# First modulation of a hybrid block: all four quarters as two TensorE rows

## The chip, the cores and the metric

The kernel runs on one core of a Trainium2 chip. The metric is the device time of one execution in microseconds (us); a lower time is better. The engines named below are PE (TensorE), DVE (VectorE), ACT (ScalarE), POOL (GpSimd) and SP (SyncE, whose queue issues the DMAs here).

## What is computed

The block works on 2048 latent tokens and 256 context tokens of width 1024. Before anything else each token is normalised and modulated; the shift and the scale are rows of 1024 numbers made from a conditioning vector, one vector `c` for the latents and one, `c_ctx`, for the context:

```python
ml = jnp.split((jax.nn.silu(c) @ p["mod_w"] + p["mod_b"])[:, None, :], 6, axis=-1)
mc = jnp.split(jax.nn.silu(c_ctx) @ p["mod_w"] + p["mod_b"], 6, axis=-1)
zl = modulate(rms_norm(xl, p["norm1_g"]), ml[0], ml[1]) @ p["w_in"]
zc = modulate(rms_norm(xc, p["norm1_g"]), mc[0], mc[1]) @ p["w_in"]
# modulate(h, shift, scale) = h * (1 + scale) + shift
```

`zl` and `zc` feed three groups of mixers (gated linear attention, a delta-rule recurrence, retention). Their outputs go through one output projection, a second normalisation and a squared-ReLU MLP. All inputs are float32.

## The kernel before

**First modulation (`modulation1`).** It needs the first 2048 columns of `mod_w`, a 1024 by 2048 matrix, in four quarters of 512 columns. Eight DMAs of 1 MB each bring them into the tiles `mw`, two for each quarter. `cs` holds SiLU of both conditioning vectors, two columns for each of the eight slices of 128 rows. Quarters 0 and 1 are the shift, quarters 2 and 3 the scale.

For quarters 0 and 1 PE multiplies the eight slices by the two columns at once (L199), which gives a tile `pm` of two rows (latents and context; one buffer); DVE adds the bias (L201, tile `mrow`), and a product with a selector `msel` (L202) spreads one of the rows over all 128 partitions (tile `pb`), from where ACT copies it to `b1r` (L203). For quarters 2 and 3 the latents go another way: DVE multiplies each of the eight slices of `mw` by its column of `cs` and adds them up in `macc` (L208, L210), and PE sums `macc` over the partitions with a matrix of ones (L211), on top of a bias product (L205). For the context, PE multiplies the same slices by a column repeated 128 times (L214). In all cases DVE then makes `m1r = (1 + scale) * g` (L219) and takes the largest absolute value of each half row (L220, tile `mx`).

From these maxima `h_factors` (L245 to L247) makes `h_s`, a number by which each normalised token is multiplied before it is split into two float16 parts.

**Token tiles (`h_stats`, `h_block`).** There are 18 tiles `x` of 128 tokens in five blocks, taken in the order block 1 (4 tiles, latents), block 0 (2 tiles, context), blocks 2, 3 and 4 (4 tiles each). At most 12 `x` are in memory. For each tile: a DMA brings `x` (L305), ACT takes the sum of squares (L307), DVE makes the reciprocal roots of a block in 13 small steps (L310, then L140 to L146), POOL (for two tiles of the first block DVE) multiplies by `m1r` (L324), DVE multiplies by the root and adds `b1r` (L325), ACT makes the float16 part `hi` with `h_s` (L328), DVE the rest `lo` (L329), and two transposing DMAs put both into the tensors `hT_hi` and `hT_lo` (L330, L331).

**Input projection (`ip_block`).** For each of three column groups L, G and k0 and each block, PE sums 24 products into `pz` (L425), of which there are two buffers, and ACT copies `pz` to `zs` (L428), which SP stores. The weights are split in the same way (`ip_weights`, L356 to L363).

**After that** come features, a long scan (roughly 600 to 2050 us), whose PE instructions are recorded by one helper line (L1068) and into which matrix products of the rest of the input projection (`pz<-rwh,rh`, `pz<-rwl,rh`) are laid as filling, then the output projection and the MLP.

**What sets the order.** Each engine executes its instructions in program order. That order isn't the order of the source: the tile framework places the instructions of all engines by a timeline that it works out at build time (L2278), so a change at the start of the program can move instructions anywhere behind it. `issue_after` adds a wait on another instruction.

Of the kernel before, what the change touches and what calls it, by code (L numbers as in the profile page):

```python
# [11 lines left out]
F32 = mybir.dt.float32  # L12
# [5 lines left out]
ALU = mybir.AluOpType  # L18
# [4 lines left out]
P = 128  # L23
D = 1024
KD = D // P
# [124 lines left out]
def modulation1(k, xp, pp, then):  # L150

    nc, tc, I = k.nc, k.tc, k.I
    cp = k.cpool
    k.cs = cs = cp.tile([P, KD, 2], F32, name="cs")
    k.h_inv = cp.tile([P, 2], F32, name="h_inv")
    k.hs = cp.tile([P, 2], F32, name="h_s")
    k.b1r = [xp.tile([P, D], F32, name=f"b1r{s}", bufs=1) for s in range(2)]
    k.m1r = [xp.tile([P, D], F32, name=f"m1r{s}", bufs=1) for s in range(2)]
    with tc.tile_pool(name="mo1", bufs=1, side="right") as m1, tc.tile_pool(name="mo2", bufs=1, side="right") as mp:
        mw = I["mod_w"].rearrange("o (k p) n -> p (o k) n", p=P)  # L160
        k.ident = cp.tile([P, P], F32, name="ident")
        make_identity(nc, k.ident)
        cr = m1.tile([16, P], F32, name="crows")
        nc.sync.dma_start(cr[0:8], I["c"].rearrange("o (r p) -> (o r) p", p=P))
        nc.sync.dma_start(cr[8:16], I["c_ctx"].rearrange("(r p) -> r p", p=P))
        mb = mp.tile([2, 2 * D], F32, name="mbrow")
        nc.sync.dma_start(mb, I["mod_b"][:, 0 : 2 * D].to_broadcast([2, 2 * D]))
        ws = []
        for q in range(4):
            for kk in range(0, KD, 4):  # L170
                w = (m1 if q < 2 else mp).tile([P, 4, 512], F32, tag="mw", name="mw", bufs=4)
                nc.sync.dma_start(w, mw[:, kk : kk + 4, 512 * q : 512 * q + 512])
                ws += [w[:, i] for i in range(4)]
        g = xp.tile([P, D], F32, name="mrowg", bufs=1)
        nc.sync.dma_start(g, I["norm1_g"].to_broadcast([P, D]))
        ones = k.ones = cp.tile([P, P], F32, name="ones")
        nc.gpsimd.memset(ones, 1.0)
        sel = m1.tile([2, 2, P], F32, name="msel")
        nc.gpsimd.tensor_copy(sel, k.ident[0:2, 0:2].unsqueeze(2).to_broadcast([2, 2, P]))
        pc = pp.tile([P, 2, KD], F32, tag="pc", name="pc", bufs=1)  # L180
        nc.tensor.transpose(pc.rearrange("p i r -> p (i r)"), cr, k.ident[0:16, 0:16])
        th = m1.tile([P, 2, KD], F32, name="sil")
        nc.scalar.activation(th, pc, AF.Tanh, scale=0.5)
        nc.vector.tensor_scalar(th, th, 0.5, 0.5, ALU.mult, ALU.add)
        nc.vector.tensor_tensor(cs.rearrange("p r i -> p i r"), th, pc, ALU.mult)
        mx = xp.tile([P, 2, 4], F32, name="mx", bufs=1)
        mm = xp.tile([P, 2, 2], F32, name="mxx", bufs=1)
        rows = {}

        def rows_of(s):  # L190
            todo = []
            for q in range(4):
                hf, mq = slice(512 * (q % 2), 512 * (q % 2) + 512), mb[:, 512 * q : 512 * q + 512]
                pb = pp.tile([P, 512], F32, tag="pb", name="pb")
                if q < 2:
                    if s == 0:
                        pm = pp.tile([2, 512], F32, tag="pm", name="pm", bufs=1)
                        for kk in range(KD):
                            nc.tensor.matmul(pm, cs[:, kk, :], ws[KD * q + kk], start=(kk == 0), stop=(kk == KD - 1))  # L199
                        rows[q] = m1.tile([2, 512], F32, tag="row", name="mrow", bufs=2)  # L200
                        nc.vector.tensor_tensor(rows[q], pm, mq, ALU.add)  # L201
                    nc.tensor.matmul(pb, sel[:, s], rows[q], start=True, stop=True)  # L202
                    nc.scalar.copy(k.b1r[s][:, hf], pb)  # L203
                else:
                    nc.tensor.matmul(pb, ones[0:1], mq[0:1], start=True, stop=False)  # L205
                    if s == 0:
                        acc = mp.tile([P, 512], F32, tag="macc", name="macc", bufs=2)
                        nc.vector.tensor_scalar(acc, ws[KD * q], cs[:, 0, 0:1], None, ALU.mult)  # L208
                        for kk in range(1, KD):
                            nc.vector.scalar_tensor_tensor(acc, ws[KD * q + kk], cs[:, kk, 0:1], acc, ALU.mult, ALU.add)  # L210
                        k.m_last = nc.tensor.matmul(pb, ones, acc, start=False, stop=True).ins  # L211
                    else:
                        for kk in range(KD):
                            nc.tensor.matmul(pb, cs[:, kk, 1:2].to_broadcast([P, P]), ws[KD * q + kk], start=False, stop=(kk == KD - 1))  # L214

                def rest(q=q, hf=hf, pb=pb):
                    r = (k.b1r if q < 2 else k.m1r)[s][:, hf]
                    if q >= 2:
                        nc.vector.scalar_tensor_tensor(r, pb, 1.0, g[:, hf], ALU.add, ALU.mult)  # L219
                    nc.vector.tensor_reduce(mx[:, s, q : q + 1], r, axis=AX.X, op=ALU.max, apply_absolute_value=True)  # L220

                if s == 0:
                    rest()
                else:
                    todo.append(rest)

            def factors():
                for f in todo:
                    f()
                nc.vector.tensor_reduce(mm[:, s], mx[:, s].rearrange("p (a b) -> p a b", a=2), axis=AX.X, op=ALU.max)  # L230
                h_factors(nc, mm[:, s, 1:2], mm[:, s, 0:1], k.h_inv[:, s : s + 1], k.hs[:, s : s + 1])

            return factors

        rows_of(0)()
        then()
        first = h_stats(k, TOK_ORDER[0], xp)
        with tc.issue_after(k.m_last):
            rest = rows_of(1)
    return first, rest  # L240


def h_factors(nc, m, b, h_inv, hs):

    nc.vector.tensor_scalar(h_inv, m, 32.0, b, ALU.mult, ALU.add)  # L245
    nc.vector.tensor_scalar(h_inv, h_inv, 1e-30, 2.0 ** -14, ALU.max, ALU.mult)
    nc.vector.reciprocal(hs, h_inv)  # L247
# [2034 lines left out]
```

## Time and profile before

| | us |
|---|---|
| three runs | 3601.03, 3632.33, 3631.42 |
| median | 3631.42 |
| profiled execution, time | 3641.55 |
| profiled execution, span from first to last instruction | 3639.4 |
| PE busy | 3362.6 (92%) |
| DVE busy | 2388.7 (66%) |
| ACT busy | 1427.0 (39%) |
| POOL busy | 685.8 (19%) |
| mean granted PE clock | 0.913 |

Busy times say how long an engine had an instruction in work. The granted clock is the share of full speed that PE was allowed in a stretch: 1.00 is 2.4 GHz, 0.50 is 1.2 GHz. In the rows further down, a timeline row gives the start, the time in us, the engine, the line, the operation with its output and inputs, how many instructions were merged (x4), and in brackets how long the engine had been idle and what released it. An instruction that had to wait for something inside its engine shows that wait as part of its time.

### The profile page before, as it was taken

The numbers are of one execution on the slowest core, as the hardware profiler recorded it, in microseconds if no ns is written. First come the engines' busy times: TensorE is split into PE (matmuls) and PEld (weight loads), VectorE is DVE, ScalarE is ACT, GpSimd is POOL, SyncE is SP. The second block draws the span as 40 slices with busy tenths as digits, with TensorE's granted clock in tenths as the row PEclk, the third lists the DMA queues.
The fourth block names the chain that finished last, engine by engine and source line by source line (L and its number), as shares of the span: only waits on it lengthen the run. The fifth ranks groups of instructions, "written<-read, shape, count | busy, mean of one in ns | idle before, by whom it ended". The sixth has DMA issues, their size and how long they took to land. (4 is left out here: it accounts for less than half of the span.)

```text
span 3639.4 us, 62904 instructions
## 1 busy us (share of the span) xinstructions
PE 3362.6 (92%) x23600; PEld 2257.2 (62%) x23600; DVE 2388.7 (66%) x5128; ACT 1427.0 (39%) x3161; POOL 685.8 (19%) x863
## 2 busy tenths in 40 slices
PE   6798999998998999999999689799999999999997
PEld 2444445666675667777676577556666666666665
DVE  7458784767865667666656378777777764454446
ACT  3355553444434464443434234444433441122113
POOL 3224442324522223323222100000000010000001
PEclk7898999999987988778998599899999999999998
DMA  7988877536645245242523168744433473232232
GB/s 229 201 242 247 251 213 209 162 99 194 167 140 135 78 126 147 68 110 92 151 77 102 57 195 229 241 176 142 172 141 136 155 228 116 90 118 93 90 102 89
DMA packets 534345, 547.09 MB, mean 150 GB/s; under 512 B 276603, under 2 KB 407494, under 8 KB 533262
## 3 DMA queue, kind: packets, MB, share of 16 engines
q1 hardware_dynamic: 534032, 542.99, 50.1%
q8 instruction: 188, 3.08, 0.3%
q14 instruction: 125, 1.02, 0.1%
HBM read 331.18 MB, written 187.55 MB: 143 GB/s over the span
## 5 line engine op out<-in xcount | busy, mean ns | idle before, releaser
L1938 PE MATMUL pu<-H,wo 128*128 128x512 f16 x2688 | 608.7, 380 | 1.2 <-DVE s L1946 1.2
L2125 DVE TENSOR_TENSOR acc<-acc,pz 128x512 f32<-128x512 f32 x512 | 348.6, 686 | 348.3 <-PE pz L2123 346.5
L1938 PEld LDWEIGHTS <-wo 128*128 128x128 f16 x2688 | 252.0, 98 | 320.4 <-issue 41.1
L2123 PE MATMUL pz<-w2h,uh 128*128 128x512 f32 x1024 | 425.2, 419 | 11.7 <-ACT uh L1965 10.5
L2123 PE MATMUL pz<-w2l,uh 128*128 128x512 f32 x1024 | 403.4, 394 | 0.0
L2123 PE MATMUL pz<-w2h,ul 128*128 128x512 f32 x1024 | 397.3, 391 | 0.4 <-DVE ul L1967 0.4
L1068 PE MATMUL pz<-rwh,rh 128*128 128x384 f16 (+1 forms) x1376 | 294.5, 345 | 12.6 <-DMA rh<-hd 6.2
L1068 PEld LDWEIGHTS <-rh 128*128 128x128 f16 x2064 | 200.9, 106 | 137.8 <-issue 37.0
L2139 POOL TENSOR_TENSOR acc<-acc,fg 128x1024 f32<-128x1024 f32 x10 | 23.6, 2377 | 1373.9 <-ACT acc L2138 1373.9
L2123 PEld LDWEIGHTS pz<-w2h,uh 128*128 128x128 f32 x1024 | 194.0, 189 | 65.6 <-ACT uh L1965 11.5
L2123 PEld LDWEIGHTS pz<-w2h,ul 128*128 128x128 f32 x1024 | 192.9, 188 | 42.8 <-DVE ul L1967 1.1
L2123 PEld LDWEIGHTS pz<-w2l,uh 128*128 128x128 f32 x1024 | 194.2, 190 | 40.1
L425 PEld LDWEIGHTS <-wh 128*128 128x128 f16 (+2 forms) x1072 | 111.5, 108 | 148.5 <-issue 40.8
L1962 ACT ACTIVATE u<-u 128x512 f32<-128x512 f32 x64 | 36.8, 623 | 402.9 <-DVE s L1956 402.9
L425 PE MATMUL pz<-hT_hi,wh 128*128 128x512 f16 (+5 forms) x536 | 125.1, 374 | 41.4 <-ACT zs L428 23.5
L1068 PE MATMUL pz<-rwl,rh 128*128 128x384 f16 (+1 forms) x688 | 146.1, 343 | 0.0
L1068 PE MATMUL pg<-Z,BK 64*128 64x128 f32 (+1 forms) x864 | 131.3, 329 | 3.8 <-issue 1.1
L1950 ACT ACTIVATE s<-pu,iv 128x512 f32<-128x512 f32 x96 | 65.2, 684 | 166.3 <-PE pu L1938 163.9
L2043 PE MATMUL pz<-woh,yh 128*128 128x512 f32 x256 | 100.9, 409 | 30.7 <-DMA x<-in_w_out_dram 22.0
L425 PE MATMUL pz<-hT_hi,wl 128*128 128x512 f16 (+5 forms) x536 | 123.4, 368 | 0.0
L425 PE MATMUL pz<-hT_lo,wh 128*128 128x512 f16 (+5 forms) x536 | 121.4, 365 | 0.0
L1068 PEld LDWEIGHTS pg<-Z,BK 64*128 64x128 f32 x864 | 111.4, 226 | 15.0 <-issue 6.9
(522 smaller groups left out, 6920.4 us busy)
## 6 DMA issues: line engine op xcount, KB each, us to landing
rh<-hd SPq DMA_DIRECT2D x86, 512.0 KB
st<-in_mlp_w_dram SPq DMA_DIRECT2D x64, 512.0 KB
w1d<-wo SPq DMA_DIRECT2D x112, 256.0 KB
wo<-w1d SPq DMA_DIRECT2D x112, 256.0 KB
x<-in_x_dram SPq DMA_DIRECT2D x32, 512.0 KB
mw<-in_mod_w_dram SPq DMA_DIRECT2D x32, 512.0 KB
w2d<-w2h SPq DMA_DIRECT2D x32, 512.0 KB
w2d<-w2l SPq DMA_DIRECT2D x32, 512.0 KB
```

Of the source, the lines that this page charges most:

```text
L425: nc.tensor.matmul(pz[:M, o : o + step], a[:, kk, 0:M], b[:, kk, t0 + o : t0 + o + step], start=(i == 0), stop=(i == 23))
L1068: return op(out, lhs, rhs, **kw)
L1938: nc.tensor.matmul(bank, W[o][:, a, kk], H[o][:, 4 * b + kk], start=(i == 0), stop=(i == 11))
L1950: nc.scalar.activation(s, product(o), AF.Copy, scale=iv)
L1962: nc.scalar.activation(r, r, AF.Relu)
L2043: nc.tensor.matmul(pz, a[:, kk], w[:, kk, 512 * hf : 512 * hf + 512], start=(kk + i == 0), stop=(kk == KD - 1 and i == 2))
L2123: nc.tensor.matmul(pz, U[q][tb][u][:, ts], W2[q][w][:, cs], start=(i == 0), stop=(i == 5))
L2125: nc.vector.tensor_add(a[:, cs], a[:, cs], pz)
L2139: nc.gpsimd.tensor_mul(a, a, fg)
```

## The change

All four quarters now take the way of quarters 0 and 1: PE makes two rows, DVE adds the bias, and PE spreads the row over the partitions, for latents and for context. The accumulation on DVE (L208, L210), the sum by ones (L211), the bias products (L205) and the context products (L214) are gone. `mrow` has four buffers in place of two; `pm` still has one. `k.m_last`, the instruction behind which the rows of the context are issued, is now the spreading product of quarter 3.

```diff
                 hf, mq = slice(512 * (q % 2), 512 * (q % 2) + 512), mb[:, 512 * q : 512 * q + 512]
+                if s == 0:
+                    pm = pp.tile([2, 512], F32, tag="pm", name="pm", bufs=1)
+                    for kk in range(KD):
+                        nc.tensor.matmul(pm, cs[:, kk, :], ws[KD * q + kk], start=(kk == 0), stop=(kk == KD - 1))
+                    rows[q] = m1.tile([2, 512], F32, tag="row", name="mrow", bufs=4)
+                    nc.vector.tensor_tensor(rows[q], pm, mq, ALU.add)
                 pb = pp.tile([P, 512], F32, tag="pb", name="pb")
+                k.m_last = nc.tensor.matmul(pb, sel[:, s], rows[q], start=True, stop=True).ins
                 if q < 2:
-                    if s == 0:
-                        pm = pp.tile([2, 512], F32, tag="pm", name="pm", bufs=1)
-                        for kk in range(KD):
-                            nc.tensor.matmul(pm, cs[:, kk, :], ws[KD * q + kk], start=(kk == 0), stop=(kk == KD - 1))
-                        rows[q] = m1.tile([2, 512], F32, tag="row", name="mrow", bufs=2)
-                        nc.vector.tensor_tensor(rows[q], pm, mq, ALU.add)
-                    nc.tensor.matmul(pb, sel[:, s], rows[q], start=True, stop=True)
                     nc.scalar.copy(k.b1r[s][:, hf], pb)
-                else:
-                    nc.tensor.matmul(pb, ones[0:1], mq[0:1], start=True, stop=False)
-                    if s == 0:
-                        acc = mp.tile([P, 512], F32, tag="macc", name="macc", bufs=2)
-                        nc.vector.tensor_scalar(acc, ws[KD * q], cs[:, 0, 0:1], None, ALU.mult)
-                        for kk in range(1, KD):
-                            nc.vector.scalar_tensor_tensor(acc, ws[KD * q + kk], cs[:, kk, 0:1], acc, ALU.mult, ALU.add)
-                        k.m_last = nc.tensor.matmul(pb, ones, acc, start=False, stop=True).ins
-                    else:
-                        for kk in range(KD):
-                            nc.tensor.matmul(pb, cs[:, kk, 1:2].to_broadcast([P, P]), ws[KD * q + kk], start=False, stop=(kk == KD - 1))
```

Behind the changed lines the line numbers of the changed kernel are 11 lower (L324 is L313, L247 is L236).

The change also moves instructions. On DVE, the place where the factor `h_s` of the latents is made (L247 before, L236 in the changed kernel). Before, these rows stand between the last maximum of the latents' scale and `h_s`:

```order
L230 TENSOR_REDUCE mxx<-mx 128x2
L310 TENSOR_SCALAR ms<-ss 128x4
L324 TENSOR_TENSOR x<-x,m1r_144 128x1024
L245 TENSOR_SCALAR h_inv<-mxx 128x1
L140 TENSOR_SCALAR rsy<-ms 128x4
L142 TENSOR_SCALAR rsh<-ms 128x4
L246 TENSOR_SCALAR h_inv<-h_inv 128x1
L141 TENSOR_SCALAR rsy<-rsy 128x4
L247 RECIPROCAL h_s<-h_inv 128x1
```

In the changed kernel the last twelve rows up to `h_s` are these (`b1r_143` and `m1r_145` are the context's rows, `wl` and `st` belong to weights):

```order
L209 TENSOR_REDUCE mx<-b1r_143 128x1
L345 MEMSET st 128x8x112
L208 SCALAR_TENSOR_TENSOR m1r_145<-pb,mrowg 128x512
L314 SCALAR_TENSOR_TENSOR x<-x,rsy,b1r_142 128x1024
L208 SCALAR_TENSOR_TENSOR m1r_145<-pb,mrowg 128x512
L235 TENSOR_SCALAR h_inv<-h_inv 128x1
L335 RECIPROCAL ar<-sc 128x1
L352 SCALAR_TENSOR_TENSOR wl<-st,sc,wh 128x8x96
L209 TENSOR_REDUCE mx<-m1r_145 128x1
L140 TENSOR_SCALAR rsy<-ms 128x4
L209 TENSOR_REDUCE mx<-m1r_145 128x1
L236 RECIPROCAL h_s<-h_inv 128x1
```

So `h_s` moved behind the modulation of the first four tiles, the context's scale rows and one weight tile; ahead of the twelve rows stand two L324, three L325 and the other small rows. The roots of the first block, which stood behind `h_s`, now stand ahead of it.

On SP, the loads of the last eight `x`. Before, four of them stood behind the first eight transposes, and the last one here:

```order
L305 DMA x<-in_x_dram 128x1024
L330 DMA_TRANSPOSE hT_hi<-hi 128x8x128 x2
L331 DMA_TRANSPOSE hT_lo<-lo 128x8x128 x3
L330 DMA_TRANSPOSE hT_hi<-hi 128x8x128
L331 DMA_TRANSPOSE hT_lo<-lo 128x8x128
L305 DMA x<-in_x_dram 128x1024
L429 DMA zc_L<-zs 96x512
```

In the changed kernel they stand together, behind the transposes of all ten tiles of blocks 1, 0 and 2:

```order
L319 DMA_TRANSPOSE hT_hi<-hi 128x8x128 x3
L320 DMA_TRANSPOSE hT_lo<-lo 128x8x128 x3
L319 DMA_TRANSPOSE hT_hi<-hi 128x8x128
L320 DMA_TRANSPOSE hT_lo<-lo 128x8x128
L294 DMA x<-in_x_dram 128x1024 x8
L418 DMA zc_L<-zs 96x512
```

So no load of the last eight `x` goes out before the twentieth transpose.

On ACT, around the copy of the first k0 block (`zs` 128x512), on which PE waits for a buffer. Before:

```order
L307 ACTIVATE sq,ss<-x 128x1024
L328 ACTIVATE hi<-x,h_s 128x1024
L307 ACTIVATE sq,ss<-x 128x1024 x3
L428 ACTIVATE zs<-pz,iv 128x512
L428 ACTIVATE zs<-pz,iv 96x256
```

In the changed kernel:

```order
L296 ACTIVATE sq,ss<-x 128x1024 x7
L317 ACTIVATE hi<-x,h_s 128x1024
L296 ACTIVATE sq,ss<-x 128x1024
L417 ACTIVATE zs<-pz,iv 128x512
L317 ACTIVATE hi<-x,h_s 128x1024
L417 ACTIVATE zs<-pz,iv 96x256
```

The copy stood and stands behind the square of the last `x`; new ahead of it is a `hi` of block 3.

## Rows read from the trace of the kernel before

**Rows 1.** Windows: stretch, length, busy (instructions) of five engines, clock, DMA share, GB/s
```profile
107.50:123.70 16.20, 0.05 (x1) 0.00 (x0) 8.54 (x6) 5.31 (x11) 10.31 (x4) 0.62 1.08 240
123.70:178.40 54.70, 54.31 (x266) 32.59 (x266) 13.35 (x21) 12.99 (x19) 3.35 (x18) 0.96 0.84 185
178.40:600.00 421.60, 388.28 (x2274) 190.06 (x2273) 292.32 (x677) 222.88 (x480) 154.14 (x193) 0.97 0.82 233
600.00:2050.00 1450.00, 1352.21 (x14235) 1005.94 (x14236) 961.99 (x2594) 619.87 (x1747) 446.80 (x609) 0.85 0.43 122
```

**Rows 2.** Timeline, 117 to 126 us: from the last load of x to PE
```profile
117.47 0.57 SPq L305 DMA_DIRECT2D x<-in_x_dram  x1
121.95 1.06 ACT L307 ACTIVATE sq<-x 128x1024 bf16<-128x1024 f32 x1 [10.10 <-DMA x<-in_x_dram]
123.01 1.03 ACT L428 ACTIVATE zs<-pz,iv 128x512 f32<-128x512 f32 x2
123.73 1.87 PE L425 MATMUL pz<-hT_hi,wh 128*112 128x256 f16 x8 [16.18 <-ACT zs L428]
```

**Rows 3.** Timeline, 0 to 40 us: the modulation on PE and DVE
```profile
16.93 0.68 DVE L201 TENSOR_TENSOR mrow<-pm,mbrow 2x512 f32<-2x512 f32 x1 [12.68 <-PE pm L199]
17.75 1.09 PE L202 MATMUL pb<-mrow,msel 2*128 2x512 f32 x2 [0.86 <-DVE mrow L201]
18.77 7.03 PE L199 MATMUL pm<-mw,cs 128*2 128x512 f32 x16
...
33.24 2.05 PE L211 MATMUL pb<-macc,ones 128*128 128x512 f32 x2
35.33 0.69 DVE L219 SCALAR_TENSOR_TENSOR m1r<-pb,mrowg 128x512 f32<-128x512 f32 x1 [0.99 <-PE pb L211]
```

**Rows 4.** Groups by line, 0 to 130 us: busy us, mean ns, idle before
```profile
L210 DVE SCALAR_TENSOR_TENSOR macc<-mw,cs,macc 128x512 f32<-128x512 f32 x14 | 10.4, 748 | 0.3
L214 PE MATMUL pb<-mw,cs 128*128 128x512 f32 x32 | 17.1, 696 | 0.0
```

**Rows 5.** Windows of the same columns as rows 1, for PE's clock
```profile
18.00:25.00 7.00, 7.00 (x17) 1.29 (x17) 5.81 (x9) 0.59 (x1) 0.00 (x0) 1.00 1.05 387
...
30.00:46.00 16.00, 16.00 (x21) 5.52 (x20) 14.61 (x22) 11.35 (x21) 7.56 (x3) 0.50 0.90 338
```

**Rows 6.** Timeline, 36 to 58 us: DVE beside POOL
```profile
36.16 5.63 POOL L324 TENSOR_TENSOR x<-x,m1r 128x1024 f32<-128x1024 f32 x2 [34.06 <-ACT sq L307]
36.66 2.93 DVE L324 TENSOR_TENSOR x<-x,m1r 128x1024 f32<-128x1024 f32 x1
...
42.68 1.21 DVE L324 TENSOR_TENSOR x<-x,m1r 128x1024 f32<-128x1024 f32 x1
...
44.07 4.66 POOL L324 TENSOR_TENSOR x<-x,m1r 128x1024 f32<-128x1024 f32 x2 [2.27 <-ACT sq L307]
...
44.14 2.31 DVE L141 TENSOR_SCALAR rsy<-rsy 128x4 int32<-128x4 int32 x1
...
46.36 0.15 DVE L247 RECIPROCAL h_s<-h_inv 128x1 f32<-128x1 f32 x1
46.48 2.26 DVE L144 TENSOR_TENSOR rst<-rsy 128x4 f32<-128x4 f32 x1
...
50.46 2.48 DVE L325 SCALAR_TENSOR_TENSOR x<-x,rsy,b1r 128x1024 f32<-128x1024 f32 x2
```

**Rows 7.** Timeline, 51 to 111 us: first split, loads of x, transposes
```profile
51.78 1.15 ACT L328 ACTIVATE hi<-x,h_s 128x1024 f16<-128x1024 f32 x1 [6.61 <-DVE x L325]
...
68.73 2.85 SPq L305 DMA_DIRECT2D x<-in_x_dram  x4
...
73.32 1.06 ACT L307 ACTIVATE sq<-x 128x1024 bf16<-128x1024 f32 x1 [5.84 <-DMA x<-in_x_dram]
...
74.75 1.06 ACT L307 ACTIVATE sq<-x 128x1024 bf16<-128x1024 f32 x1 [0.28 <-DMA x<-in_x_dram]
...
110.64 4.00 SPq L331 DMA_TRANSPOSE hT_lo<-lo  x3
```

## The prediction

> **What bounds the kernel now.** Read the windows first. From 123.7 to 178.4 us PE is busy for 54.3 of 54.7 us, from there to 600 us for 388 of 422, in the scan for 1352 of 1450 [rows 1]. So PE bounds nearly everything behind 123.7 us, and its work there isn't touched by the change. In the 16.2 us before that PE is idle [rows 1]. The timeline says why, read backwards [rows 2]: PE waits 16.18 us for a buffer `pz`, which ACT frees with the copy `zs` at 123.01; ACT was stuck from 111.85 on in front of the square of the last `x`, which came at 121.95 because SP issued its load only at 117.47. The question is thus not how much work the change saves, but when this copy runs. I call the start of PE at 123.73 the restart; what it delays or brings forward goes to the end of the kernel, as far as PE's order behind it stays the same.
>
> **The work removed and added.** DVE loses 14 multiply-adds, 10.4 us, and two first products; PE loses 32 instructions for the context, 17.1 us [rows 4], and small sums and bias products. PE gains 32 instructions of the two-row kind: 16 for each quarter, 7.03 us at 1.00 of the clock [rows 3, 5]. None of the removed work stands on the chain of rows 2, so its sum (some 28 us) is no gain by itself: PE did the context at a time when it had nothing else, and DVE built `macc` while PE worked on quarters 0 and 1.
>
> **Step 1, when the latents' scale is ready.** Before, the last `m1r` of the latents ends at 35.33 + 0.69 = 36.0 us [rows 3]. In the changed kernel four quarters follow one another on PE, because `pm` has one buffer and because the spreading product stands between them in program order. One turn: from the end of a quarter (about 16.9) to the start of the next (18.77) it is 1.9 us, in which the bias is added (0.68) and the row is spread (1.09); then 7.03 us of products; together 8.9 us [rows 3]. The first quarter ends at 16.9, so the fourth ends at 16.9 + 3 x 8.9 = 43.6; 1.9 us for its row and 0.9 us for `m1r` give 46.4. That is 10.4 us later than before. The data isn't what is late: before, DVE had summed over all of `mw` when PE took the last sum at 33.24 [rows 3]. I take the clock at 1.00, as it was in the like stretch from 18 to 25 us; from 30 to 46 us PE stood at 0.50 [rows 5], and at 0.50 for the last two quarters the step would cost another 14 us (32 x 7.03 / 16).
>
> **Step 2, when `h_s` is ready.** Before it is there at 46.5 us, and the first `hi` starts at 51.78 [rows 6, 7]. Now the order puts 26 DVE instructions between `m1r` and `h_s`, and POOL has eight products `x*m1r` next to them. In the rows a POOL product and a DVE instruction with two inputs don't run together: L324 takes 1.21 us alone and 2.93 beside POOL; L141 and L144, four numbers wide, take 2.31 and 2.26 beside two POOL products of 2.33, against 0.15 for L247 that fell between those two [rows 6]. So while POOL has products ready, DVE gets one instruction through between two of them. The Trainium skill (SBUF — State Buffer, Who interferes with whom) calls this an exclusive lock, held for a whole instruction, in which the loser fully blocks. The trace agrees with it, by the 2.31 us just shown; by that rule the sum is the upper one below, and if the two engines only shared a bandwidth it would lie between the two.
> The sum: the first six POOL products, 6 x 2.33 = 14.0, and the two L324 in between, 2 x 1.21, make 16.4. Then DVE is alone for four L325 (4 x 1.24), two maxima and two `m1r` of the context (512 wide like L201 and L219, 4 x 0.69), a memset (at most an L324, 1.2) and four small ones (0.15), about 9.6; then the two POOL products of the context with a small one between, 4.8; a weight rest `wl` (1.2), two maxima, two or three small ones, 3.1. Together 33.9: `h_s` at 46.4 + 33.9 = 80.3 us. The lower bound is DVE's own time: two L324 2.4, four L325 5.0, seven instructions of 512 elements 4.8, memset and `wl` 2.4, twelve small ones 1.8, together 16.4, which gives 62.8.
>
> **Step 3, when the last `x` are loaded.** All eight loads now stand behind twenty transposes. The first needs a `hi` (1.15), and SP takes 4.00 / 3 = 1.33 us for each [rows 7]: 80.3 + 1.2 + 26.6 = 108.1. DVE has about 22 us of large work in the same time (ten `lo` and six L325 at 1.24, two `wl`), so it just keeps up. A load lands 4.6 us after its issue and the next 1.43 later (68.73 to 73.32 and 74.75) [rows 7]: the first square starts at 112.7, the eighth `x` is there at 122.7. That is nearly the moment of before, by chance: the later start is made up by loading in one piece.
>
> **Step 4, the restart.** Ahead of the copy on ACT there now also stands a `hi` of block 3, which needs the roots of that block and L325 on DVE, and behind it the square of the eighth `x`. POOL multiplies the seven tiles whose squares stand ahead of that `hi`, from 113.8 on, back to back: 7 x 2.33 = 16.3, until 130.1. The 13 steps of the root depend on one another, begin at about 118 and pass one at a time between POOL's products, so about 8 are left at 130.1: 1.6 us with their gaps. Then L325 1.24, `hi` 1.15, the square 1.06, the copy 0.72 [rows 2, 6, 7]: 135.9. Before, the restart was at 123.7, so it comes 12 us later. If DVE and POOL cost each other nothing in steps 2 and 4, `h_s` at 62.8 brings the first square to 95.2; the seventh ends 9.6 us later, and `hi`, the eighth square and the copy take 2.9: 107.7, which is 16 us earlier than before. Those are the ends: -16 and +12, and +26 with the clock of step 1 at 0.50. I take +12, since the rows in which a DVE instruction stands still beside POOL are all those of rows 6, and it is by them that the step is made.
>
> **Step 5, to the end.** At the restart PE has the same work left as before, G and k0 of the context (half a block each) and three column groups of blocks 2 to 4, 54.7 us [rows 1], 5.5 for one. Block 3 is needed at 135.9 + 4 x 5.5 = 158 us and block 4 at 174; their `hi` begin at 133, and 16 transposes of 1.33 end at about 155, so no new wait. The features and the scan start 12 us later and keep their length; cover of 12 us isn't there, as PE idles only 33 us of 422 in many pieces before the scan. Sum against the profiled execution: 3641.55 + 12 = 3653.6, 0.33% more. On the median of the three runs, 3631.42, that is 3643.4. The profiled execution lay 10 us above that median, so I keep to the difference.
>
> **The rivals.**
> (a) The front becomes faster. The removed 11 us of DVE and 17 us of PE come through: DVE finds gaps between POOL's products, and `h_s` comes near 63 us. For it speaks that the two engines slow each other only while POOL has a tile ready; against it the rows of 2.3 us [rows 6]. 3631 - 16 = 3615.
> (b) PE's clock stands at 0.50 in quarters 2 and 3. For it speaks that it did so from 30 us on before; against it that PE had less to do then than now, when only the turns of 1.9 us break its products, as between quarters 0 and 1, where it kept 1.00 [rows 3, 5]. 3631 + 26 = 3657.
> (c) Slower by more than can be put down to the front: the filling products of the scan (`pz<-rwh,rh`, `pz<-rwl,rh`, L1068) lie up to some 400 places later in PE's new order, so that in parts of the scan PE has less to fill its waits with, and its clock goes down there. The mean clock of the scan is 0.85 [rows 1]; at 0.83 its 1352 us of PE cost 1352 x 0.02 / 0.83 = 33 us, with the front 45: 3676. It decides from a loss of about 25 us in the scan on, and no row bounds it; in the order the places have evened out again before the scan's end.
> (d) The same in the other direction: the new order suits the scan better, at a clock of 0.87. With the front +12 this gives 3612 (1352 x 0.02 / 0.87 = 31), and with (a) 3584.
> (e) Nothing reaches the end, because the last copy isn't what frees PE: 3631. Against it speak the 16.18 us of rows 2.
>
> **How the numbers follow.** Less than 1% either way (3595 to 3668) is about what a measurement of this kernel tells from no change. My forecast, +12 within a few us, 0.52; (a) 0.16; (b) 0.08; (c) 0.12; (d) 0.08; (e) 0.04. The time is that of the forecast, 3643. The likeliest case alone spans 3636 to 3651. For 8 in 10 the range goes down past (a) and (d) with the spread of the runs before (3601 at the lowest) and up past (b) to short of (c): 3606 to 3670. Faster by over 1% needs (d) with (a), or more than (d), 0.05; slower by over 1% is (c) and a little of (b), 0.13; within 1% 0.82.
>
> **What would show it.** Last `m1r` of the latents at 46 us rather than 36; `h_s` near 80; small DVE instructions of 2.3 us beside POOL; the eight loads of `x` at about 108 us in a row; the copy of the k0 block and PE's restart near 136; from there 55 us of dense PE. The forecast is wrong if `h_s` is there by 70 us, if PE restarts before 124, or if the time from 600 to 2050 us differs by more than 15 us.

## The result

| kernel | median us (runs) | ratio to before, 95% interval |
|---|---|---|
| before, beside the changed kernel | 3633.16 (20) | 1 |
| changed kernel | 3656.41 (20) | 1.0055 [1.0028, 1.0081] |
| changed kernel, a second time beside before at 3623.85 (19) | 3651.38 (12) | 1.0061 [1.0033, 1.0089] |

The changed kernel is slower by half a per cent, some 20 us. The medians are over all executions; the ratios leave out, in either kernel, the slow executions that lie more than 1.5% above its fastest (four of the changed kernel's first 20). It was profiled twice, in executions of 3690 and 3666 us; the lines here are of the second, which is nearer to the median (its span is 3663.9 us). Its line numbers are smaller than those of before, by 1 or 2 in the modulation and by 11 behind it.

The timeline of the modulation, where [rows 3, 6] stood for before; columns: start, duration, engine, line, what is computed, idle time before it.

```profile
18.70 7.03 PE L197 MATMUL pm<-mw,cs 128*2 128x512 f32 x16
...
36.40 7.03 PE L197 MATMUL pm<-mw,cs 128*2 128x512 f32 x16
44.20 1.12 PE L201 MATMUL pb<-mrow,msel 2*128 2x512 f32 x2 [0.77 <-DVE mrow L199]
...
45.35 0.69 DVE L208 SCALAR_TENSOR_TENSOR m1r<-pb,mrowg 128x512 f32<-128x512 f32 x1 [0.76 <-PE pb L201]
...
46.19 17.76 POOL L313 TENSOR_TENSOR x<-x,m1r 128x1024 f32<-128x1024 f32 x6 [44.09 <-DVE ar L329]
46.74 6.16 DVE L313 TENSOR_TENSOR x<-x,m1r 128x1024 f32<-128x1024 f32 x2
52.95 2.17 DVE L299 TENSOR_SCALAR ms<-ss 128x4 f32<-128x4 f32 x1
55.04 9.99 DVE L314 SCALAR_TENSOR_TENSOR x<-x,rsy,b1r 128x1024 f32<-128x1024 f32 x3
...
69.83 5.47 POOL L313 TENSOR_TENSOR x<-x,m1r 128x1024 f32<-128x1024 f32 x2 [5.88 <-DVE h_inv L235]
...
71.32 1.71 DVE L140 TENSOR_SCALAR rsy<-ms 128x4 int32<-128x4 int32 x1
...
73.54 0.15 DVE L236 RECIPROCAL h_s<-h_inv 128x1 f32<-128x1 f32 x1
```

The last `m1r` of the latents ends at 46.0 us instead of 36.0 [rows 3], and `h_s` is there at 73.7 instead of 46.5 [rows 6]. The way from there to TensorE's restart, which answers [rows 2, 7]:

```profile
103.28 4.23 SPq L294 DMA_DIRECT2D x<-in_x_dram  x8
...
107.26 1.06 ACT L296 ACTIVATE sq<-x 128x1024 bf16<-128x1024 f32 x1 [8.55 <-DMA x<-in_x_dram]
...
108.48 16.15 POOL L313 TENSOR_TENSOR x<-x,m1r 128x1024 f32<-128x1024 f32 x7 [33.18 <-ACT sq L296]
...
113.19 2.27 DVE L140 TENSOR_SCALAR rsy<-ms 128x4 int32<-128x4 int32 x1
...
124.69 0.16 DVE L144 TENSOR_TENSOR rst<-rsy 128x4 f32<-128x4 f32 x1
...
125.95 7.02 DVE L314 SCALAR_TENSOR_TENSOR x<-x,rsy,b1r 128x1024 f32<-128x1024 f32 x4
...
127.27 1.15 ACT L317 ACTIVATE hi<-x,h_s 128x1024 f16<-128x1024 f32 x1 [10.71 <-DVE x L314]
...
129.36 0.67 ACT L417 ACTIVATE zs<-pz,iv 128x512 f32<-128x512 f32 x1
...
130.08 1.86 PE L414 MATMUL pz<-hT_hi,wh 128*112 128x256 f16 x8 [23.35 <-ACT zs L417]
...
145.08 3.36 PE L414 MATMUL pz<-hT_hi,wh 128*112 128x512 f16 x8 [1.99 <-ACT zs L417]
```

The windows that answer [rows 1, 5], of PE alone; columns: stretch, length, busy (instructions), granted clock, DMA share, GB/s.

```profile
107.50:123.70 16.20, 0.00 (x0) 0.61 0.84 293
123.70:178.40 54.70, 46.19 (x218) 0.86 0.79 162
178.40:600.00 421.60, 384.00 (x2226) 0.96 0.82 233
600.00:2050.00 1450.00, 1342.96 (x14182) 0.86 0.44 124
...
30.00:46.00 16.00, 14.46 (x34) 1.00 0.78 305
```

PE restarts at 130.1 instead of 123.7, and from 123.7 to 178.4 us it is busy for 46 us instead of 54. From 600 to 2050 us its busy time and its clock are those of before to about 1%, though the span is 24 us longer. A view by fixed windows doesn't tell where they went. For that I use three marks which every kernel has: the restart; the start of the fourth column group (the first wide product behind the wait for its weights `wh`); and the scan's own 864 products `pg<-Z,BK`, their first and last start. The view of one line gives the last mark (min/median/max ns, first and last start, shapes); before, then changed:

```profile
L1068 PE MATMUL pg<-Z,BK x864: 270/272/579, 606.3 to 1916.0; 64*128 64x128 f32 x154, 64*128 64x64 f32 x19
```
```profile
L1057 PE MATMUL pg<-Z,BK x864: 270/272/580, 626.1 to 1943.7; 64*128 64x128 f32 x154, 64*128 64x64 f32 x19
```

These products start 19.8 us later and end 27.7 us later. In the other profile of the same kernel they ran from 626.5 to 1973.5: the same start, and an end 30 us later. So the front repeats within 1 us from one execution to the next, and the scan doesn't. The last of these products isn't the end of the scan: PE still has products of the retention behind them, and the first product of the output projection comes at 2095.8 us before and at 2119.4 us in the changed kernel, 23.6 us later. I use this as a fourth mark.

### The profile page after: what moved, and what is told of

Its sections match the earlier page's. It is cut to its first block, busy times and chain, and to the rows that moved or that the text cites. A ratio compares the mean times of both kernels' runs of the same rounds, so it can differ in the third digit from the quotient of the medians.

```text
span 3688.5 us, 62930 instructions
## 1 busy us (share of the span) xinstructions
PE 3376.4 (92%) x23596; PEld 2259.5 (61%) x23596; DVE 2380.8 (65%) x5114; ACT 1425.8 (39%) x3161; POOL 682.3 (18%) x863
```

## The experiments

Theory A is that of the prediction: the front is late, and the lateness goes to the end. Theory B: the time is decided behind the front, by the order that the instructions of the scan get, since the scheduler lays them anew with every edit.

All marks and ratios first; "length" is from the first to the last start of the 864 products, "output" the start of the first product of the output projection. The marks are of one profiled execution of each kernel, and executions of one kernel differ (before: 3601 to 3664 us), so they don't rank the kernels behind the front. "Clock" is the granted clock of an execution, averaged over the executions that the ratio is made of, and ratios are to runs of before on the same chip (three chips, on which before had 0.918, 0.919 and 0.917).

| kernel | fourth group | scan's products | length | output | clock | ratio, 95% interval |
|---|---|---|---|---|---|---|
| before | 181.4 | 606.3 to 1916.0 | 1310 | 2095.8 | 0.918 | 1 |
| changed (second profile) | 191.6 | 626.1 to 1943.7 | 1318 | 2119.4 | 0.920 | 1.0061 [1.0033, 1.0089] |
| context half alone | 192.6 | 619.1 to 1953.4 | 1334 | 2139.0 | 0.916 | 1.0115 [1.0079, 1.0150] |
| latents half alone | 193.2 | 625.6 to 1937.4 | 1312 | 2100.1 | 0.921 | 1.0100 [1.0067, 1.0133] |
| changed, `h_s` first | 184.2 | 611.4 to 1956.2 | 1345 | 2138.7 | 0.915 | 1.0066 [1.0037, 1.0095] |
| changed, products on DVE | 178.7 | 591.3 to 1953.8 | 1363 | 2126.2 | 0.915 | 1.0074 [1.0042, 1.0106] |
| changed, products on DVE behind `h_s` | 161.0 | 596.4 to 1913.2 | 1317 | 2066.4 | 0.925 | 0.9947 [0.9918, 0.9976] |
| the same again | 160.4 | 592.1 to 1923.4 | 1331 | 2072.1 | 0.924 | 0.9961 [0.9927, 0.9996] |
| before, products on DVE behind `h_s` | 155.6 | 588.7 to 1901.5 | 1313 | 2072.3 | 0.918 | 1.0014 [0.9984, 1.0043] |
| before + 4 copies | 181.8 | 606.6 to 1938.5 | 1332 | 2101.7 | 0.921 | 1.0019 [0.9986, 1.0052] |
| before + 32 copies | 181.9 | 607.2 to 1903.5 | 1296 | 2063.9 | 0.922 | 0.9986 [0.9948, 1.0024] |
| changed + 4 copies | 191.2 | 623.5 to 1915.5 | 1292 | 2083.2 | 0.917 | 1.0081 [1.0050, 1.0112] |
| changed, `h_s` first, + 4 copies | 182.8 | 610.8 to 1907.4 | 1297 | 2063.0 | 0.925 | 0.9932 [0.9900, 0.9965] |

In every profile of the table the output projection and what follows it take 1537 to 1547 us, so what separates the profiles has happened before that mark.

**The changed kernel again.** Nothing is edited.

> The changed kernel itself, once more, for a profile beside the other kernels of this chip. My theory (the front is late by the last m1r at 46.6 us, by h_s behind the products and the eight late x loads, and the delay is carried to the end): last m1r 46.6, h_s 74, first square of block 3 at 108, PE restart 130.5, end of the first three column groups 189, then the rest as before plus 7 to 20 us: 3640 to 3655 us. Rival (the new order of the instructions makes the scan itself slower): end of the input projection 15 to 20 us late and the scan a further 10 to 30 us late at an equal granted clock, 3665 us and over.

Measured: `m1r` 46.0, `h_s` 73.7, first square 107.3, restart 130.1, end of the third group 10.2 us late, time 3651. The front came as expected, and the time lies in the range of my theory; the lateness at the end of the input projection (19.8) is also what the rival named. This run alone decides nothing.

**The context's half alone.**

```
...
-                    nc.tensor.matmul(pb, ones[0:1], mq[0:1], start=True, stop=False)
                     if s == 0:
+                        nc.tensor.matmul(pb, ones[0:1], mq[0:1], start=True, stop=False)
...
                     else:
+                        pm = pp.tile([2, 512], F32, tag="pm", name="pm", bufs=1)
                         for kk in range(KD):
-                            nc.tensor.matmul(pb, cs[:, kk, 1:2].to_broadcast([P, P]), ws[KD * q + kk], start=False, stop=(kk == KD - 1))
+                            nc.tensor.matmul(pm, cs[:, kk, :], ws[KD * q + kk], start=(kk == 0), stop=(kk == KD - 1))
+                        rows[q] = m1.tile([2, 512], F32, tag="row", name="mrow", bufs=4)
+                        nc.vector.tensor_tensor(rows[q], pm, mq, ALU.add)
+                        nc.tensor.matmul(pb, sel[:, 1], rows[q], start=True, stop=True)
```

> Only the context's half of the change: its quarters 2 and 3 come from two rows by TensorE, the latents' quarters 2 and 3 are accumulated by VectorE as before. The same result is computed. My theory (the latents' late m1r and h_s make the cost): last latents' m1r at 36 to 38 us and h_s at 47 to 58 as before; the eight x loads stand behind all 20 transposes in this order too, but those start some 18 us earlier than in the changed kernel, so first square 88 to 100, PE restart at 108 to 124, end of the three column groups at or before 179, time 3615 to 3640. Rival (a new order of the whole program costs, whatever the front does): front as above, yet 3640 to 3660. Rival (context's half alone is what costs): restart at 130 or later although h_s is early.

Measured: `h_s` at 46.6 us and the first `hi` at 51.8, as expected, and yet the restart at 130.8, which only the last of the three expectations had named; the time is 3672 us. The timeline and the waits of SP's queue (us in total, times, longest) tell why:

```profile
62.01 0.67 DVE L217 TENSOR_TENSOR mrow<-pm,mbrow 2x512 f32<-2x512 f32 x1
62.74 2.07 PE L218 MATMUL pb<-mrow,msel 2*128 2x512 f32 x2 [15.46 <-DVE mrow L217]
...
SPq L334 <- PE pb L218: 14.0, 1, 14.0
```

DVE adds the context's third row only at 62.01, behind the work on `x`; PE stands in front of it for 15.5 us, and the fourth row follows at 74.6. The transposes of `hi`, ready since 53 us, wait for that product: `hT` takes the place of the modulation's weights and rows (both are pools of the right side). I had not seen that the transposes depend on the last reader of the weights. So this half costs the front 11 us by a way of its own, which the whole change doesn't take, since there all four rows are made by 44.1 us.

**The latents' half alone.**

```
                 if s == 0:
                     pm = pp.tile([2, 512], F32, tag="pm", name="pm", bufs=1)
...
-                k.m_last = nc.tensor.matmul(pb, sel[:, s], rows[q], start=True, stop=True).ins
+                if s == 0 or q < 2:
+                    k.m_last = nc.tensor.matmul(pb, sel[:, s], rows[q], start=True, stop=True).ins
+                else:
+                    nc.tensor.matmul(pb, ones[0:1], mq[0:1], start=True, stop=False)
+                    for kk in range(KD):
+                        nc.tensor.matmul(pb, cs[:, kk, 1:2].to_broadcast([P, P]), ws[KD * q + kk], start=False, stop=(kk == KD - 1))
```
(+ and - are against the changed kernel.)

> Only the latents' half of the change: the latents' quarters 2 and 3 come from two rows by TensorE, the context's from eight broadcast matmuls each as before. The same result is computed. Here h_s stands behind two VectorE products and four scale-and-adds, but no longer behind the context's m1r; four x loads are issued behind the first eight transposes, the other four behind the rest; and the copy that TensorE waits for stands ahead of the squares on ScalarE. My theory: last m1r 46 to 47, h_s at 62 to 74, and since the copy no longer waits for the last x, PE restarts at 95 to 118, so the end of the three column groups is at 165 to 185 and the time 3615 to 3640, less than the changed kernel though m1r is as late. Rival (a late m1r and h_s cost by themselves, whatever the order behind them): restart at 130, time as the changed kernel, 3640 to 3655. Rival (new order of the scan): front early, time 3640 to 3660.

Measured: last `m1r` 45.8, `h_s` 69.4, both as expected, but the restart at 136.8:

```profile
126.43 2.00 SPq L299 DMA_DIRECT2D x<-in_x_dram  x4
...
136.24 0.81 ACT L422 ACTIVATE zs<-pz,iv 96x256 f32<-96x256 f32 x2
...
136.75 1.87 PE L419 MATMUL pz<-hT_hi,wh 128*128 128x256 f16 x8 [25.68 <-ACT zs L422]
```

The copy that I had found ahead of the squares did run early; PE then stopped further on, at the next copy, which stands behind four squares whose `x` was loaded at 126.4. Moving one copy ahead only moves the stop to the next. The fourth group is late by 11.8 us and the time longer by 1%; none of the expectations had this.

**The changed kernel with `h_s` first.**

```
+                k.hs_last = nc.cur_bb.bb.instructions[-1]
...
+        with k.tc.issue_after(k.hs_last) if stats else ExitStack():
-        (nc.vector if stats and i % 2 else nc.gpsimd).tensor_mul(x, x, k.m1r[s])
+            (nc.vector if stats and i % 2 else nc.gpsimd).tensor_mul(x, x, k.m1r[s])
```

> The changed kernel with one edge more: VectorE's products of x with m1r are queued behind the reciprocal that makes the latents' h_s, so that the small instructions of h_s come first. The same result is computed. My theory: last m1r 46.6 as in the changed kernel, h_s at 47 to 50 in place of 74, first hi at about 58 to 62, the x loads of block 3 in three parts between transposes from about 75 on, first square 80 to 95, PE restart 100 to 120, end of the three column groups 160 to 182, time 10 to 25 us below the changed kernel. Rival (what costs is the new order of the rest and not the front): the front as above and the time within 5 us of the changed kernel.

Measured: `h_s` at 52.0 (a small instruction beside POOL took 2.25 us), first `hi` at 61.9, loads of `x` at 82.8, 93.5 and 95.9, the last long stop of PE over at 125.9, fourth group at 184.2: 7.4 us of the 10.2 are back, a little less than expected. The time isn't: 3649 us, ratio 1.0066. By my theory that couldn't be; the rival had it.

**Products on DVE, with and without `h_s` first.** Two kernels, each the changed one with the line of the product replaced:

```
-        (nc.vector if stats and i % 2 else nc.gpsimd).tensor_mul(x, x, k.m1r[s])
+        nc.vector.tensor_mul(x, x, k.m1r[s])
```
and the same within `with k.tc.issue_after(k.hs_last):`, with `k.hs_last` set as above.

> The changed kernel with all products of x with m1r on VectorE, order otherwise left to the scheduler: h_s stands behind eight products and no longer behind GpSimd. The same result is computed. Small VectorE instructions no longer take 2.25 us each, since no GpSimd product runs beside them: the block-3 root takes 2 to 3 us in place of 12. Front: h_s 66 to 75, first square of block 3 at 98 to 108, restart 112 to 122 against 130.5. Theory A: 8 to 18 us below the changed kernel. Theory B: no tie to the front; of all kernels with a new order this one moves the scan least (54 places in the middle against 221), so if the order of before is the favourable one it comes nearest to before, 3625 to 3650.

> The changed kernel with all products of x with m1r on VectorE, queued behind the reciprocal that makes the latents' h_s, so that GpSimd takes no part in the front. The same result is computed. Front: last m1r 46.6, h_s 47 to 48, first hi at 56 to 58, restart of TensorE no later than 118, so 12 us ahead of the changed kernel. Its scan has the most displaced order of all (460 places on average in one stretch). Theory A: 10 to 18 us below the changed kernel, 3630 to 3640, at or near before. Theory B: the front's gain is not seen in the end; 3640 to 3675, whatever the restart.

Measured, the first: `h_s` 71.4, first square 104.6, restart 116.2, all as expected. The steps of the block-3 root take 0.15 us, since no GpSimd product is beside them:

```profile
112.55 0.15 DVE L144 TENSOR_TENSOR rst<-rsy 128x4 f32<-128x4 f32 x1
...
116.20 1.86 PE L414 MATMUL pz<-hT_hi,wh 128*112 128x256 f16 x8 [11.00 <-ACT zs L417]
```

The scan starts 15 us earlier than in before and its last product comes 38 us later, in a profiled execution of 3669 us that is the longest of its 12; ratio 1.0074. The second:

```profile
47.29 0.15 DVE L237 RECIPROCAL h_s<-h_inv 128x1 f32<-128x1 f32 x1
...
70.49 2.02 SPq L295 DMA_DIRECT2D x<-in_x_dram  x4
...
89.25 2.01 SPq L295 DMA_DIRECT2D x<-in_x_dram  x4
...
160.99 4.45 PE L416 MATMUL pz<-hT_hi,wh 128*128 128x512 f16 x16 [1.70 <-ACT wh L353]
```

PE has no stop of more than 8 us left behind 60 us; the fourth group starts 20.4 us before that of before. This kernel takes 3604.87 us and is faster than both, 0.9947, and below what either theory had given (3630 us and up). Its executions had a mean clock of 0.925, those of before beside them 0.919. It was run a second time, beside before with the same edit.

**Another order of the scan, with nothing else.** The scheduler lays the scan's fillers by the times it reckons; a few tiny instructions on ScalarE (128x1 copies) between the front and the scan make it choose another order.

```
-            rw_seg(k, p0)
+            rw_seg(k, p0); z = p0.tile([P, 1], F32, name="scrap", bufs=1); [nc.scalar.copy(z, k.h_inv[:, 0:1]) for _ in range(4)]
```

> The kernel before, with nothing of the change, and four copies of one column more on ScalarE (128x1 into a spare tile, about 0.2 us each) behind the setting up of the scan's segments. The result is computed as before. The front up to TensorE's row 1203 (about 300 us) keeps its order; behind it the scheduler lays the fillers of the scan otherwise, by 119 places on average and 406 at most in the middle of the scan (the change moves them by 221 and 476 there). Theory A (the change costs because its front is late and the delay is carried): front as before, restart 123 to 125, and the time as before within 5 us, ratio 0.998 to 1.002. Theory B (the order of the scan is what costs, since the kernel before has a favourable one, and the granted clock in the scan follows it): front as before and the time 10 to 40 us above it, ratio 1.003 to 1.011, lost between 600 and 2050 us.

> As the kernel with four copies, but with 32 of them (together some 6 us on ScalarE, which is idle 60 percent of the time there), which gives a third order of the scan: 239 places on average and 582 at most in its second half. Theory A: ratio to before 0.998 to 1.002, since the front is that of before. Theory B: ratio 1.003 to 1.011 with a loss between 600 and 2050 us, of another size than with four copies, because it is another order.

Measured: fronts as in before, ratios 1.0019 and 0.9986, both with 1 inside. So a new order isn't bad by itself, and by these two before wasn't an unusually lucky one. Theory B in the form "any other order costs" falls.

> The changed kernel with four copies of one column more on ScalarE behind the setting up of the scan's segments (0.2 us each): the first 2000 rows of TensorE keep the changed kernel's order, the fillers of the scan behind them move by 138 places on average. The same result is computed. Theory A (the late front is what costs): the front as in the changed kernel, fourth column group from 190 to 192, and the ratio to before 1.003 to 1.009 again. Theory B (the scan's order decides by itself): the same front and a ratio that may be anywhere from 0.997 to 1.012; a value below 1.002 would say that the changed kernel's cost came with its scan and not with its front.

> The changed kernel with h_s ahead of the products (its front is 3 us behind the kernel before at the fourth column group, its time 0.66 percent above it), with the four copies, which give it another order of the scan. The same result is computed. Theory A: its front is near before, so with another scan it comes near before: ratio 0.998 to 1.003, and the 0.66 percent came with the scan. Theory B': something of the front that the profile marks do not show costs 20 us in every such kernel: ratio 1.004 to 1.010 again.

Measured: the changed kernel stays slow with the other order, 1.0081. But the kernel with `h_s` first goes from 1.0066 to 0.9932 by these four copies, at a front that differs by 1.4 us. The rows of the scan's products, without and with the copies:

```profile
L1059 PE MATMUL pg<-Z,BK x864: 270/272/580, 611.4 to 1956.2; 64*128 64x128 f32 x154, 64*128 64x64 f32 x19
```
```profile
L1059 PE MATMUL pg<-Z,BK x864: 272/272/579, 610.8 to 1907.4; 64*128 64x128 f32 x154, 64*128 64x64 f32 x19
```

The order of the scan alone is thus worth 1.3% between two kernels, which neither expectation had (0.998 at the lowest). Where they part, by windows of PE from the first product of the scan to the first one of the output projection; without the copies, then with them:

```profile
611.40:2138.70 1527.30, 1398.46 (x14262) 0.82 0.42 119
```
```profile
610.80:2063.00 1452.20, 1320.82 (x14261) 0.87 0.45 125
```

The instructions are as many, and PE is idle for 129 and 131 us. What differs is the time for which PE is busy with them, and the clock, 0.82 against 0.87. These 75 us are more than the order is worth: the profiled execution of the first is the longest of its eight (3679 us), that of the second lies near its median. Over all executions the two clocks are 0.915 and 0.925. Two stretches, of PE and then of the products that fill the scan (`pz<-rwh,rh` and `pz<-rwl,rh`, all instructions on the tile `rh`); without the copies:

```profile
1440.00:1480.00 40.00, 36.55 (x273) 0.51 0.59 143
...
1440.00:1480.00 40.00, 0.61 (x2) 0.51 0.59 143
```

and with them:

```profile
1520.00:1560.00 40.00, 40.00 (x319) 0.50 0.15 42
...
1520.00:1560.00 40.00, 0.00 (x0) 0.50 0.15 42
```

The slow kernel has 40 us at the low clock with two filling products in them, but the fast one has such 40 us too, with none. Why the one order keeps the higher clock over the whole scan, these windows don't show.

**Before with the same edit, and the faster kernel again.**

> The kernel before, without the change, with the edit that made the changed kernel faster: all products of x with m1r on VectorE, queued behind the reciprocal of the latents' h_s. The same result is computed. It tells what the change itself is worth when both have the good front. Theory A: the last m1r is again 10 us earlier (36 against 46.6), h_s at 43 to 46, first hi at 51 to 55, fourth column group at 150 to 158 against 161, time 5 to 10 us below the changed kernel with this edit: ratio to before 0.990 to 0.995. Theory B (order of the scan): time anywhere from 3595 to 3660 whatever its front.

> The changed kernel with all products on VectorE behind h_s, once more, on the chip of the kernel before with the same edit. Ratio to before 0.992 to 0.998 again, fourth column group at 161; it is 5 to 10 us above the kernel before with the same edit if the late m1r costs what it showed in the front (theory A), equal to it or either way if the scan decides (theory B).

Measured on one chip: before with the edit 3628.71 us, 1.0014; changed with the edit 3610.38 us, 0.9961. Before has the better front of the two, by 4.8 us at the fourth group, as expected, and is not the faster one. The front doesn't rank these two. Nor does before gain by a front that is 26 us better than its own without the edit, at nearly the same clock (0.918 against 0.917): in the profile its scan starts 17.6 us earlier, and PE is idle in the scan for 145 us instead of 129.

## Why the prediction was right, and where not

**Step 1 was right.** 46.4 us were reckoned for the last `m1r`, 46.0 came (46.6 in the first profile). The turns of 8.9 us are there: quarters start at 18.70, 27.55 and 36.40. The clock stood at 1.00 from 30 to 46 us, so rival (b), in which it stood at 0.50 there, is out.

**Step 2 had the right mechanism and was 6.6 us too long:** `h_s` at 73.7, reckoned 80.3, lower bound 62.8. Two terms failed. One is the four L325 "alone" behind the six products: three of them (L314 now) passed between POOL's products, 9.99 us for three, so that the stretch behind the six products, reckoned at 9.6 us, took 5.9. The other is the stretch with the context's two POOL products, reckoned at 7.9 us: it took 3.9, from 69.8 to 73.7, since one small instruction (L140, 1.71 us) waited there and not two products' time went by. Against these 7.7 us stand 1.2 by which the six products themselves ended later than reckoned. What the Trainium skill says (SBUF — State Buffer, Who interferes with whom), that the loser waits for a whole instruction, is seen once more in the 2.17 us of an L299 of four columns beside POOL, and in the 0.15 us of a step of the root, four columns too, once GpSimd has no product.

**Step 3 and 4 were right in length.** From `h_s` to the issue of the eight loads 29.6 us (27.8 reckoned), from the first square to the restart 22.8 us (23.2 reckoned). The steps of the root pass at 2.27 us, one to a product. The restart at 130.1 is 6.4 us later than before instead of 12.2, by what step 2 had too much.

**Step 5 is where the reckoning went wrong.** First half, "so no new wait": PE waits another 1.99 us for `zs` at 145.08 and runs the next eight products in 3.36 us, and the three groups end 10.2 us late. Then come the 9.6 us from the fourth group to the scan's start; PE in this stretch, before and changed:

```profile
181.40:606.30 424.90, 392.33 (x2299) 0.97 0.82 233
```
```profile
191.60:626.10 434.50, 397.37 (x2299) 0.96 0.80 229
```

For the same 2299 instructions PE is idle for 4.6 us longer and busy for 5.0 us longer. One wait grew by 7.1 us, the one for DVE in front of the features (3.5 us in three waits before, 10.6 us in four now), and others became shorter. Over the kernels of the table the lateness at the fourth group is found again at the scan's start within 11 us, but for the one with products on DVE (fourth group 2.7 us early, scan 15 us early). So up to there a late front is carried, and in the changed kernel it even doubles.

Second half, "the scan keeps its length": that holds in the second profile of the changed kernel and not in the first. From the first product of the scan to the first one of the output projection, before, then changed in the second profile, then in the first:

```profile
606.30:2095.80 1489.50, 1360.64 (x14262) 0.84 0.43 122
```
```profile
626.10:2119.40 1493.30, 1353.90 (x14261) 0.85 0.43 122
```
```profile
626.50:2143.90 1517.40, 1377.98 (x14261) 0.83 0.43 120
```

PE is idle in it for 129 us before and for 139 in both profiles of the changed kernel, so 10.5 us of idle time are new; the rest is time at work, shorter by 6.7 us where the clock was 0.85 and longer by 17 where it was 0.83. So the 24.5 us of the second profile are 19.8 at the scan's start, 10.5 of idle time in the scan, 6.7 less at work, and 0.9 behind the scan.

Rivals (c) and (d) put the decision into the clock of the scan; I gave them 0.12 and 0.08 and let neither into the number. Between executions of one kernel the clock does decide: in before and in the changed kernel alike an execution is some 30 us shorter for each 0.01 more of its granted clock (an estimate, from a straight line through the 19 and the 12 executions on one chip). But the clock isn't what makes the changed kernel slower. On that chip its executions had 0.920 and took 3647.2 us on average, those of before 0.918 and 3623.5 us. So (c) isn't what happened: from 600 to 2050 us the second profile has a clock of 0.86, before has 0.85, and (c) had reckoned with 0.83. The changed kernel does have a stretch such as (c) describes, in both profiles; of PE and then of the filling products:

```profile
1260.00:1280.00 20.00, 20.00 (x141) 0.50 0.19 53
...
1260.00:1280.00 20.00, 0.50 (x1) 0.50 0.19 53
```

But before has one as well, only later:

```profile
1260.00:1280.00 20.00, 20.00 (x237) 1.00 0.54 119
...
1260.00:1280.00 20.00, 1.49 (x7) 1.00 0.54 119
...
1520.00:1540.00 20.00, 20.00 (x182) 0.50 0.06 18
...
1520.00:1540.00 20.00, 0.00 (x0) 0.50 0.06 18
```

From 1260 to 1320 us the changed kernel runs almost only the scan's small products, at a clock of 0.50 (1.2 GHz). Before it fell the fillers had stopped, and before it rose to 1.00 (2.4 GHz) at 1325 us they had come back. That the one is the reason of the other isn't shown: before kept 1.00 from 1260 to 1280 with 1.49 us of fillers.

**Why the number was nearly right all the same.** Forecast were 12 us more than before, measured 0.28 to 0.81%, 10 to 29 us. The 19.8 us at the scan's start would be 0.54%. That 12 came so near is in part luck: step 2 was 6.6 us too long, while the 13.4 us that PE lost from the restart to the scan's start and the 10.5 us of idle time in the scan stood at nothing in the sum. And that the late front is what reaches the end of every execution is not shown. For it speaks that all four kernels with a fourth group at 191 us or later are slow, by 0.55 to 1.15%, whichever order their scan has, and the changed one at a clock no lower than that of before; against it that two kernels with a front about as good as that of before are as slow (1.0066, 1.0074, though both at the lower clock of 0.915), that one with nearly the same front is faster by 0.7% (at a clock of 0.925), and that before with a front 26 us earlier isn't faster at all. A test would need two fronts with one and the same order of the scan, and a resolution of some 0.2%; the orders differed with every change of the front that I found large enough.

## What to carry to other kernels

A delay of 10 us at the head of a kernel whose order a scheduler lays by reckoned times is less than what the new order itself can do: here the same front gave 1.0066 and 0.9932. Before a change of a few tenths of a per cent is judged, give both kernels another order or two (a few tiny instructions between the stages) and look whether the verdict stays; and put the granted clock of the executions beside their times, which tells a loss by late starts and waits, as in the changed kernel, from one by the clock. And at the head of such a kernel the order in which an engine takes its instructions can matter more than the work that is saved: the 10 and 17 us taken from VectorE and TensorE brought nothing, while products moved behind a three-instruction chain (`h_s`) and off GpSimd moved the fourth group forward by 30 us. That kernel beats both, but it isn't shown that it does so by its front: its executions also had the higher clock, and before with the same edit has the earlier front still and isn't faster than before.

## What the runs showed of the hardware that I had not expected

- PE's clock stood at 0.50 from 1260 to 1320 us while PE was recorded as busy for 20.00 of each 20 us, and in the first profile of the changed kernel likewise from 1255 to 1310; in before it stood at 0.50 from 1520 to 1560 us in the same way. The Trainium skill (TensorE: Matmul & The Clock Gate, HAM oscillation) tells of clocks that fall in waits for data; here the stretch at 0.50 has no wait in the records, whose ends of products are modelled.
- One and the same program had a scan of 1318 and 1347 us in two executions, with a front that agreed within 1 us; the clock over the whole was 0.914 and 0.908.
- Four tiny copies on an engine that isn't the bound, 0.19 us each, moved the time of one kernel by 1.3% through the order that the scheduler chose (those of two others by 0.2%, within the intervals).
